# Sixteen batched matmuls: casting loads on GpSimd's queue, replaced by plain fp32 loads and stores on one hardware queue with casts on VectorE

## The chip, the cores and the metric

The kernel runs on one NeuronCore of a Trainium2 chip. The metric is the device time of one execution in microseconds. Three executions of the kernel before took 276.04, 276.12 and 276.22 us; their median is 276.12 us. The profiled execution has a span of 276.1 us from its first to its last instruction.

Engine names in the profile: PE is TensorE (PEld its weight loads), DVE is VectorE, ACT is ScalarE, POOL is GpSimd, SP is SyncE. A trailing "q" (SPq, POOLq) means the sequencer of an engine, which issues DMAs. L49 is line 49 of the kernel file.

## The reference

```python
def setup_inputs():
    batch, m, k, n = 16, 512, 768, 1024
    return {
        "x": np.random.randn(batch, k, m).astype(np.float32),
        "y": np.random.randn(batch, k, n).astype(np.float32),
    }

def reference(x, y):
    return np.einsum('bkm,bkn->bmn', x, y).astype(np.float32)
```

For each of 16 batches, x (768 x 512) is contracted with y (768 x 1024) over the first axis, and the result is 512 x 1024, all of it fp32 in HBM. Per batch 1.573 MB of x and 3.146 MB of y are read and 2.097 MB of the result are written: 6.816 MB, and 109.05 MB over the 16 batches. The sum over k may be taken in any order, so any assignment of the 768 rows to partitions is allowed as long as x and y have the same one.

## The kernel before

The matmuls run in bf16 with fp32 sums in PSUM. K = 768 is cut into KT = 6 slices of 128 rows, M = 512 into MT = 4 tiles of 128, N = 1024 into NT = 2 tiles of 512. One batch is 6 x 4 x 2 = 48 matmuls of 128x512, each with its own weight load of 128x128.

**Loads.** GpSimd issues four DMAs for each batch (L62 and L64, two halves of three K slices of x and of y). They read fp32 rows from HBM and cast to bf16 on the way into SBUF. Row ko*128 + p goes to partition p, so a contiguous run of x is one row of 512 elements (2 KB in HBM, 1 KB in SBUF), and one of y a row of 1024 elements (4 KB and 2 KB). x_sb and y_sb have four buffers each, so loads run up to four batches ahead.

**Matmuls.** With K_OUTER the loop over K slices is the outer one: all eight PSUM banks of a batch are open at the same time, and the 48 matmuls go through them six times (L49, called from L73). The first bank is complete only after most of the batch.

**Copies and stores.** When a batch's matmuls are done, its eight PSUM banks are copied to SBUF as fp32, alternately by VectorE and ScalarE (L78). After every second copy SyncE issues a store of one 128 x 1024 tile (512 KB, L79), in which a contiguous run is one output row of 4 KB. So there are four stores per batch, on SyncE's hardware queue, beside the loads on GpSimd's software queue. Both queues are served by the same 16 DMA engines.

The order is the scheduler's; on each engine the instructions stand in program order, and each DMA waits on its issuing queue for the semaphores it needs.

Of the kernel before, what the change touches and what calls it, by code (L numbers as in the profile page):

```python
# [1 line left out]

_os.environ.setdefault("NEURON_RT_ULTRASERVER_MODE", "4")

# [1 line left out]

# [4 lines left out]

LOAD_SPLIT = 2
K_OUTER = True


@with_exitstack
def kernel(
    ctx: ExitStack,
    tc: tile.TileContext,  # L20
    x: bass.AP,
    y: bass.AP,
    out: bass.AP,
):
    nc = tc.nc
    P = 128
    FP32 = mybir.dt.float32
    BF16 = mybir.dt.bfloat16

    B, K, M = x.shape  # L30
    _, _, N = y.shape

    KT = K // P
    MT = M // P
    NF = 512
    NT = N // NF
    KC = KT // LOAD_SPLIT

    x_v = x.rearrange("b (ko p) m -> b ko p m", p=P)
    y_v = y.rearrange("b (ko p) n -> b ko p n", p=P)  # L40
    o_v = out.rearrange("b (mo p) n -> b mo p n", p=P)

    x_pool = ctx.enter_context(tc.tile_pool(name="x_pool", bufs=4))
    y_pool = ctx.enter_context(tc.tile_pool(name="y_pool", bufs=4))
    o_pool = ctx.enter_context(tc.tile_pool(name="o_pool", bufs=12))
    psum = ctx.enter_context(tc.tile_pool(name="psum", bufs=8, space=bass.MemoryType.PSUM))

    def mm(ps, x_sb, y_sb, kt, mt, nt):
        nc.tensor.matmul(  # L49
            ps[:],  # L50
            x_sb[:, kt, mt * P:(mt + 1) * P],
            y_sb[:, kt, nt * NF:(nt + 1) * NF],
            start=(kt == 0),
            stop=(kt == KT - 1),
        )

    for b in range(B):
        x_sb = x_pool.tile([P, KT, M], BF16, name="x_sb")
        y_sb = y_pool.tile([P, KT, N], BF16, name="y_sb")
        for c in range(LOAD_SPLIT):  # L60
            ks = slice(c * KC, (c + 1) * KC)
            nc.gpsimd.dma_start(  # L62
                x_sb[:, ks], x_v[b, ks].rearrange("ko p m -> p ko m"))
            nc.gpsimd.dma_start(  # L64
                y_sb[:, ks], y_v[b, ks].rearrange("ko p n -> p ko n"))

        o_sb = [o_pool.tile([P, N], FP32, name="o_sb") for _ in range(MT)]
        ps = [psum.tile([P, NF], FP32, name="ps") for _ in range(MT * NT)]
        if K_OUTER:
            for kt in range(KT):  # L70
                for mt in range(MT):
                    for nt in range(NT):
                        mm(ps[mt * NT + nt], x_sb, y_sb, kt, mt, nt)  # L73
            for mt in range(MT):
                for nt in range(NT):
                    j = mt * NT + nt
                    eng = nc.vector.tensor_copy if j % 2 == 0 else nc.scalar.copy
                    eng(o_sb[mt][:, nt * NF:(nt + 1) * NF], ps[j][:])  # L78
                nc.sync.dma_start(o_v[b, mt], o_sb[mt][:])  # L79
        else:  # L80
            for mt in range(MT):
                for nt in range(NT):
                    j = mt * NT + nt
                    for kt in range(KT):
                        mm(ps[j], x_sb, y_sb, kt, mt, nt)
                    eng = nc.vector.tensor_copy if j % 2 == 0 else nc.scalar.copy
                    eng(o_sb[mt][:, nt * NF:(nt + 1) * NF], ps[j][:])
                nc.sync.dma_start(o_v[b, mt], o_sb[mt][:])


# [1 line left out]
_INS = ['x', 'y']  # L92
_OUTS = [((16, 512, 1024), 'float32')]


# [23 lines left out]
```

## Time and profile before

| | |
|---|---|
| median of three executions | 276.12 us |
| span of the profiled execution | 276.1 us |
| PE busy | 192.3 us (70%), 753 matmuls recorded of 768 |
| DVE / ACT busy | 39.7 us (14%) / 34.1 us (12%) |
| software queue q0 (casting loads) | 25600 packets, 37.75 MB written to SBUF, 75.7% of 16 engines' span |
| hardware queue q1 (stores) | 9216 packets, 33.56 MB, 32.2% |
| HBM read / written | 75.50 MB / 33.55 MB |
| mean granted TensorE clock | 0.895 |

The queue rows count bytes on the side that is written. A casting load reads twice what it writes, so the 37.75 MB of q0 are 75.50 MB read from HBM. To compare rates before and after, a GB/s number of a stretch with loads has to be brought back to HBM bytes: times 2 where only loads run, and times 109.05/71.31 = 1.529 in the steady mixture of loads and stores (71.31 MB is the sum of q0 and q1). Shares of a queue can add up to more than 100%, because the time of one packet overlaps that of the next one on the same engine.

### The profile page before, as it was taken

The page shows a single profiled execution, that of the slowest core. Times are in us where ns is not written, and L with a number is a line of the kernel's source. Part 1 is how long each engine was busy: PE and PEld are TensorE (multiplying, and loading weights), DVE is VectorE, ACT ScalarE, POOL GpSimd, SP SyncE. Part 2 cuts the span into 40 slices and gives each one's busy share as a digit, 9 for nine tenths or more (in the row PEclk, how much of TensorE's full clock was granted, in tenths as well). Part 3 has the DMA queues.
Part 4 walks back from the last instruction along what each step waited for, and adds up shares of the span by engine and source line. Part 5 has one row for each costly group of instructions (what it writes and reads, how often), then busy time and mean ns, then how long its engine had stood idle before and what let it go on. Part 6 is the DMA issues. An engine that isn't in the chain of part 4 may idle for free.

```text
span 276.1 us, 2127 instructions
## 1 busy us (share of the span) xinstructions
PE 192.3 (70%) x753; PEld 79.9 (29%) x768; DVE 39.7 (14%) x64; ACT 34.1 (12%) x65; POOL 49.8 (18%) x68
## 2 busy tenths in 40 slices
PE   0599727698278788495784993769919695849770
PEld 0144313243133333132331441324403332313330
DVE  0003110033003003030300303003030030302011
ACT  1002110022002002020200202002020020202011
POOL 8422121221212122121212311122112221000000
PEclk9999977799689979889978898689986998997997
DMA  5999999999999999999999999999999999999937
GB/s 92 202 208 237 317 279 284 208 243 315 296 268 210 284 279 245 315 210 297 260 294 267 211 302 286 319 216 209 320 291 302 209 252 309 223 315 233 283 156 304
DMA packets 34826, 71.44 MB, mean 259 GB/s; under 512 B 2048, under 2 KB 14336, under 8 KB 34816
## 3 DMA queue, kind: packets, MB, share of 16 engines
q0 software_dynamic: 25600, 37.75, 75.7%
q1 hardware_dynamic: 9216, 33.56, 32.2%
q8 instruction: 6, 0.10, 0.1%
q14 instruction: 4, 0.03, 0.0%
HBM read 75.50 MB, written 33.55 MB: 395 GB/s over the span
## 4 chain that ended last, share of the span: by engine, by line
DMA 90%; issue 3%; POOL 2%; PE 2%; DVE 0%; DVEq 0%; POOLq 0%
DMA x_sb<-in_x_dram 78%; DMA y_sb<-in_y_dram 12%; PE ps L49 2%; POOL x_sb L62 1%; POOL y_sb L64 1%; DVE o_sb L78 0%; DVEq L114 0%; DVEq L78 0%; POOLq L114 0%; POOLq L103 0%
## 5 line engine op out<-in xcount | busy, mean ns | idle before, releaser
L49 PE MATMUL ps<-y_sb,x_sb 128*128 128x512 bf16 x753 | 192.3, 416 | 77.0 <-DMA y_sb<-in_y_dram 72.3
L49 PEld LDWEIGHTS <-x_sb 128*128 128x128 bf16 x768 | 79.9, 105 | 188.8 <-issue 109.9
L78 DVE COPY o_sb<-ps 128x512 f32<-128x512 f32 x64 | 39.7, 683 | 230.6 <-issue 167.7
L78 ACT COPY o_sb<-ps 128x512 f32<-128x512 f32 x64 | 32.9, 600 | 235.2 <-issue 172.9
L64 POOL DMA_DIRECT2D y_sb<-in_y_dram x32 | 24.7, 773 | 105.2 <-DMA y_sb<-in_y_dram 105.2
L62 POOL DMA_DIRECT2D x_sb<-in_x_dram x32 | 24.8, 777 | 76.5 <-DMA x_sb<-in_x_dram 70.7
L78 ACT ACT_TABLE_LOAD x1 | 1.3, 1283 | 0.7 <-PEq L103 0.7
L103 POOL MEMSET const-float32-0.0<- 128x1 f32 x1 | 0.1, 93 | 0.2 <-issue 0.2
L103 POOL MEMSET const-bfloat16-1.0<- 128x1 bf16 x1 | 0.1, 95 | 0.0
L103 POOL MEMSET const-float32-1.0<- 128x1 f32 x1 | 0.1, 93 | 0.0
L103 POOL MEMSET const-uint8-127<- 128x1 uint8 x1 | 0.1, 93 | 0.0
## 6 DMA issues: line engine op xcount, KB each, us to landing
out_dram<-o_sb SPq DMA_DIRECT2D x64, 512.0 KB, 8.9
y_sb<-in_y_dram POOLq DMA_DIRECT2D x32, 768.0 KB, 32.9
x_sb<-in_x_dram POOLq DMA_DIRECT2D x32, 384.0 KB, 32.8
```

Source lines behind the costliest of these rows:

```text
L49: nc.tensor.matmul(ps[:], x_sb[:, kt, mt * P:(mt + 1) * P], y_sb[:, kt, nt * NF:(nt + 1) * NF], start=(kt == 0), stop=(kt == KT - 1),)
L62: nc.gpsimd.dma_start(x_sb[:, ks], x_v[b, ks].rearrange("ko p m -> p ko m"))
L64: nc.gpsimd.dma_start(y_sb[:, ks], y_v[b, ks].rearrange("ko p n -> p ko n"))
L78: eng(o_sb[mt][:, nt * NF:(nt + 1) * NF], ps[j][:])
L103: nc = _bacc.Bacc("TRN2", target_bir_lowering=False, num_devices=1)
```

## The change

The change rewrites how data gets in and out, and hands the cast to an engine.

- **Loads** are plain fp32 DMAs into staging tiles xs and ys (two buffers each), one DMA for x and one for y per batch, issued by SyncE (L56, L57). Row p*6 + ko goes to partition p, so each partition reads one contiguous run: 12 KB of x, 24 KB of y.
- **Casts** to bf16 are on VectorE: one for x (L62) and two halves for y (L65), each 128 x 3072 elements. x_sb and y_sb now have two buffers each.
- **Matmuls** (L74) have the K slices innermost, one PSUM bank at a time. Weights are taken at a step of four elements (x_w, L66), so that output row j*4 + mo lands on partition j, and a partition's four output rows are one contiguous run of 16 KB.
- **PSUM copies** are all on ScalarE (L76), into an o_sb tile of a whole batch, of which there are five.
- **Stores** are one DMA per batch (L50, 2 MB), on the same SyncE queue as the loads, and batch b-4 is stored right behind the loads of batch b. The last four batches are stored after the last loads.
- The order is fixed by hand (`tc.manual_schedule()`): every engine runs its instructions as written.

```diff
-    x_v = x.rearrange("b (ko p) m -> b ko p m", p=P)
-    y_v = y.rearrange("b (ko p) n -> b ko p n", p=P)
-    o_v = out.rearrange("b (mo p) n -> b mo p n", p=P)
-    x_pool = ctx.enter_context(tc.tile_pool(name="x_pool", bufs=4))
-    y_pool = ctx.enter_context(tc.tile_pool(name="y_pool", bufs=4))
-    o_pool = ctx.enter_context(tc.tile_pool(name="o_pool", bufs=12))
+    x_v = x.rearrange("b (p ko) m -> b p ko m", ko=KT)
+    y_v = y.rearrange("b (p ko) n -> b p ko n", ko=KT)
+    o_v = out.rearrange("b (p mo) n -> b p mo n", mo=MT)
+    xs_pool = ctx.enter_context(tc.tile_pool(name="xs_pool", bufs=2))
+    ys_pool = ctx.enter_context(tc.tile_pool(name="ys_pool", bufs=2))
+    x_pool = ctx.enter_context(tc.tile_pool(name="x_pool", bufs=2))
+    y_pool = ctx.enter_context(tc.tile_pool(name="y_pool", bufs=2))
+    o_pool = ctx.enter_context(tc.tile_pool(name="o_pool", bufs=5))
+    LAG = 4
...
+    def store(b):
+        nc.sync.dma_start(o_v[b], o_tiles.pop(b)[:])
+
+    with tc.manual_schedule():
+        for b in range(B):
+            xs = xs_pool.tile([P, KT, M], FP32, name="xs")
+            ys = ys_pool.tile([P, KT, N], FP32, name="ys")
+            nc.sync.dma_start(xs[:], x_v[b])
+            nc.sync.dma_start(ys[:], y_v[b])
+            if b >= LAG:
+                store(b - LAG)
+            x_sb = x_pool.tile([P, KT, M], BF16, name="x_sb")
+            y_sb = y_pool.tile([P, KT, N], BF16, name="y_sb")
+            nc.vector.tensor_copy(x_sb[:], xs[:])
+            for h in range(2):
+                ks = slice(h * KT // 2, (h + 1) * KT // 2)
+                nc.vector.tensor_copy(y_sb[:, ks], ys[:, ks])
+            x_w = x_sb[:].rearrange("p k (j mo) -> p k mo j", mo=MT)
+            o_sb = o_pool.tile([P, MT, N], FP32, name="o_sb")
+            o_tiles[b] = o_sb
+            for mo in range(MT):
+                for nt in range(NT):
+                    ns = slice(nt * NF, (nt + 1) * NF)
+                    ps = psum.tile([P, NF], FP32, name="ps")
+                    for kt in range(KT):
+                        nc.tensor.matmul(ps[:], x_w[:, kt, mo], y_sb[:, kt, ns],
+                                         start=(kt == 0), stop=(kt == KT - 1))
+                    nc.scalar.copy(o_sb[:, mo, ns], ps[:])
...
+        for b in sorted(o_tiles):
+            store(b)
```

How the order of the instructions changes is seen at three places. In the rows, DMAHW and DMASW are semaphores that a DMA raises when it has landed (eight of each kind, used in turn), and DVE, PE and Activation are those of the engines.

The first place is the middle of the program on the queues that issue DMAs. Before, GpSimd issues the loads of two batches like this, with none of the stores among them:

```order
L62 DMA x_sb_379<-in_x_dram 128x3x512 [waits DMASW0_49,PE_49]
L64 DMA y_sb_380<-in_y_dram 128x3x1024 [waits DMASW1_49]
L62 DMA x_sb_379<-in_x_dram 128x3x512 [waits DMASW2_49]
L64 DMA y_sb_380<-in_y_dram 128x3x1024 [waits DMASW3_49]
L62 DMA x_sb_457<-in_x_dram 128x3x512 [waits DMASW4_49,PE_49]
L64 DMA y_sb_458<-in_y_dram 128x3x1024 [waits DMASW5_49]
```

A load there waits for the one eight DMAs earlier, whose semaphore it reuses, and at the start of a batch for TensorE to be done with the buffer. With the change, SyncE's queue holds everything; here are the loads of batches 4 and 5 and the stores of batches 0 and 1:

```order
L56 DMA xs_371<-in_x_dram 128x3072 [waits DMAHW4_49,DVE_49]
L57 DMA ys_372<-in_y_dram 128x6144 [waits DMAHW5_49,DVE_49]
L50 DMA out_0_dram<-o_sb_84 128x4096 [waits Activation_49]
L56 DMA xs_446<-in_x_dram 128x3072 [waits DMAHW6_49,DVE_49]
L57 DMA ys_447<-in_y_dram 128x6144 [waits DMAHW7_49,DVE_49]
L50 DMA out_0_dram<-o_sb_158 128x4096 [waits Activation_49]
```

A load now waits for VectorE to have cast the batch two before out of the same staging buffer, and a store, which waits for ScalarE's copies of the batch four before, stands between the loads.

The second place is the end of SyncE's queue with the change: the last loads (batch 15) and the stores of batches 11 to 15.

```order
L56 DMA xs_1196<-in_x_dram 128x3072 [waits DMAHW3_49,DVE_49]
L57 DMA ys_1197<-in_y_dram 128x6144 [waits DMAHW4_49,DMAHW2_49,DVE_49]
L50 DMA out_0_dram<-o_sb_906 128x4096 [waits Activation_49]
L50 DMA out_0_dram<-o_sb_981 128x4096 [waits Activation_49]
L50 DMA out_0_dram<-o_sb_1056 128x4096 [waits DMAHW5_49,Activation_49]
L50 DMA out_0_dram<-o_sb_1131 128x4096 [waits DMAHW6_49,Activation_49]
L50 DMA out_0_dram<-o_sb_1206 128x4096 [waits DMAHW7_49,Activation_49]
```

Five whole batches' stores now stand behind the last load; before, it was the stores of the batch just computed.

The third place is the start of a batch's casts on VectorE with the change (batches 1 and 2), where before there were only copies out of PSUM:

```order
L62 CAST x_sb_153<-xs_149 128x3072 [waits DMAHW2_49]
L65 CAST y_sb_154<-ys_150 128x3072 [waits DMAHW3_49]
L65 CAST y_sb_154<-ys_150 128x3072
L62 CAST x_sb_227<-xs_223 128x3072 [waits DMAHW4_49,DVE_49,PE_49]
L65 CAST y_sb_228<-ys_224 128x3072 [waits DMAHW5_49,DVE_49]
```

A cast waits for its load to have landed, and from the third batch on for TensorE to be done with the bf16 buffer of the batch two before.

More of the change, by code (lines that the diff above doesn't have):

```diff
@@ L11 @@
 from concourse._compat import with_exitstack
-LOAD_SPLIT = 2
-K_OUTER = True
 @with_exitstack
@@ L36 @@
     NT = N // NF
-    KC = KT // LOAD_SPLIT
-    x_v = x.rearrange("b (ko p) m -> b ko p m", p=P)
-    y_v = y.rearrange("b (ko p) n -> b ko p n", p=P)
-    o_v = out.rearrange("b (mo p) n -> b mo p n", p=P)
-    x_pool = ctx.enter_context(tc.tile_pool(name="x_pool", bufs=4))
-    y_pool = ctx.enter_context(tc.tile_pool(name="y_pool", bufs=4))
-    o_pool = ctx.enter_context(tc.tile_pool(name="o_pool", bufs=12))
-    psum = ctx.enter_context(tc.tile_pool(name="psum", bufs=8, space=bass.MemoryType.PSUM))
@@ L48, in mm @@
[L48 to L74, printed above, removed]
-                for nt in range(NT):
[L76 to L83, printed above, removed]
-                    for kt in range(KT):
[L85 to L88, printed above, removed]
@@ new lines @@
+    psum = ctx.enter_context(tc.tile_pool(name="psum", bufs=8, space=bass.MemoryType.PSUM))
+    LAG = 4
+    o_tiles = {}
+    def store(b):
[18 more added lines that the diff above has]
+            for mo in range(MT):
+                for nt in range(NT):
+                    ns = slice(nt * NF, (nt + 1) * NF)
+                    ps = psum.tile([P, NF], FP32, name="ps")
+                    for kt in range(KT):
+                        nc.tensor.matmul(ps[:], x_w[:, kt, mo], y_sb[:, kt, ns],
+                                         start=(kt == 0), stop=(kt == KT - 1))
+                    nc.scalar.copy(o_sb[:, mo, ns], ps[:])
+            if False:
+                store(b)
+        for b in sorted(o_tiles):
+            store(b)
```

## The prediction

> **What bounds the kernel now.** I read the page first: busy shares, DMA rows, queues, and the shares of the chain of waits.
>
> ```profile
> span 276.1 us, 2127 instructions
> ...
> PE 192.3 (70%) x753; PEld 79.9 (29%) x768; DVE 39.7 (14%) x64; ACT 34.1 (12%) x65; POOL 49.8 (18%) x68
> ...
> DMA  5999999999999999999999999999999999999937
> ...
> DMA packets 34826, 71.44 MB, mean 259 GB/s; under 512 B 2048, under 2 KB 14336, under 8 KB 34816
> ...
> q0 software_dynamic: 25600, 37.75, 75.7%
> q1 hardware_dynamic: 9216, 33.56, 32.2%
> q8 instruction: 6, 0.10, 0.1%
> ...
> HBM read 75.50 MB, written 33.55 MB: 395 GB/s over the span
> ...
> DMA 90%; issue 3%; POOL 2%; PE 2%; DVE 0%; DVEq 0%; POOLq 0%
> ```
>
> The DMA engines are busy in every slice but the first and the last two, and 90% of the chain that ended last is DMA. TensorE is busy in 70% of the span. The kernel moves 109.05 MB of HBM data and is bound by moving it, so two things matter: the rate while the DMA engines work, and how long they stand still. The next view cuts the span into stretches (columns: length, busy time of PE, PEld, DVE, ACT and POOL, PE clock, DMA share, GB/s by written bytes).
>
> ```profile
> 12.00:20.00 8.00, 8.00 (x35) 3.50 (x34) 0.00 (x0) 0.00 (x0) 2.32 (x3) 1.00 1.14 208
> 40.00:238.00 198.00, 146.26 (x564) 60.17 (x573) 29.00 (x47) 24.08 (x48) 35.95 (x47) 0.88 1.12 267
> ...
> 270.00:274.00 4.00, 0.00 (x0) 0.00 (x0) 0.29 (x1) 0.07 (x1) 0.00 (x0) 0.87 1.02 406
> ```
>
> *Rate.* From 12 to 20 us only loads run: 208 GB/s written, 416 read. From 270 to 274 only stores: 406. In the steady middle 267 x 1.529 = 408 GB/s of HBM bytes. All three are within 3%, on one queue or on two.
>
> *Standing still.* The same view at the two ends of the program, and the rows of the timeline that belong to it:
>
> ```profile
> 3.00:4.00 1.00, 0.00 (x0) 0.00 (x0) 0.00 (x0) 0.00 (x0) 1.00 (x2) 1.00 0.26 40
> 4.00:5.00 1.00, 0.00 (x0) 0.00 (x0) 0.00 (x0) 0.00 (x0) 1.00 (x2) 1.00 1.20 199
> ```
> ```profile
> 264.00:266.00 2.00, 2.00 (x10) 0.87 (x9) 0.00 (x0) 0.00 (x0) 0.00 (x0) 1.00 0.46 188
> 266.00:268.00 2.00, 1.95 (x10) 0.89 (x10) 0.19 (x1) 0.00 (x0) 0.00 (x0) 1.00 0.00 0
> 268.00:269.00 1.00, 1.00 (x6) 0.38 (x4) 1.00 (x2) 0.98 (x3) 0.00 (x0) 1.00 0.00 0
> 269.00:270.00 1.00, 0.23 (x2) 0.00 (x0) 1.00 (x3) 1.00 (x3) 0.00 (x0) 1.00 0.57 229
> ...
> 274.00:275.00 1.00, 0.00 (x0) 0.00 (x0) 0.00 (x0) 0.00 (x0) 0.00 (x0) 0.50 0.64 246
> ```
> ```profile
> 0.73 1.28 ACT L78 ACT_TABLE_LOAD   x1 [0.73 <-PEq L103]
> 1.24 0.89 POOL L62 DMA_DIRECT2D x_sb<-in_x_dram  x1 [0.80 <-POOLq L103]
> ```
> ```profile
> 263.89 5.34 PE L49 MATMUL ps<-y_sb,x_sb 128*128 128x512 bf16 x23 [3.08 <-DMA y_sb<-in_y_dram]
> ```
> ```profile
> 268.63 2.88 SPq L79 DMA_DIRECT2D out_dram<-o_sb  x4
> ```
>
> Load data begins at about 3.75 us (share 0.26 in the fourth microsecond). The last load has landed at 263.9; stores of the batch before run on until 264.9 (0.46 of two us). Then nothing moves until 269.43 (share 0.57), because the last 23 matmuls and the copies come first. The last stores end at 274.64, the span at 276.1. Idle: 3.75 + 4.5 + 1.4 = 9.7 us, which leaves 266.4 us for 109.05 MB: 409 GB/s, the steady rate again. So **276.1 = 266.4 of transfer + 9.7 idle**, and this span is the median 276.12 within 0.02, so nothing has to be added.
>
> **The change part by part.**
>
> *Bytes.* None are removed: 75.50 MB in, 33.55 MB out. The casting DMA had to read fp32 too.
>
> *Idle ends.* Head: SyncE can issue from about 0.73, when the other engines have left the start-up barrier (the table load's row). Its last group of stores was issued at 268.63 and moved at 269.43, 0.8 us later; GpSimd's first load took 3.75 - 1.24 = 2.5. With SyncE's nearer to 0.8, and something for HBM reads, I take 1.3: data at 2.0 instead of 3.75. Tail: after the last load the queue holds stores 11 to 14, 8.39 MB, some 19.6 us of transfer at the rate found below. Meanwhile the last batch needs two y casts, 48 matmuls at 146.26/564 = 0.259 us (12.4), one copy, and 0.8 from issue to data. The prices of these:
>
> ```profile
> L49 PE MATMUL ps<-y_sb,x_sb 128*128 128x512 bf16 x753 | 192.3, 416 | 77.0 <-DMA y_sb<-in_y_dram 72.3
> L49 PEld LDWEIGHTS <-x_sb 128*128 128x128 bf16 x768 | 79.9, 105 | 188.8 <-issue 109.9
> L78 DVE COPY o_sb<-ps 128x512 f32<-128x512 f32 x64 | 39.7, 683 | 230.6 <-issue 167.7
> L78 ACT COPY o_sb<-ps 128x512 f32<-128x512 f32 x64 | 32.9, 600 | 235.2 <-issue 172.9
> ```
>
> A cast is 128x3072. No row shows one; six times the 683 ns of a 512-wide copy gives 4.1 us as its upper bound, and nothing is the lower one. Then the last store is ready 13.8 to 22.0 us after y lands, against 19.6 us of stores that cover it (up to 1.4 less, as landing is seen late): a gap of 0 to 3.8 us. I take 1.5. The Trainium skill, "VectorE: DVE Perf Modes", section on the perf-mode tier table, gives 1227 ns for an fp32 copy of 2048 elements within SBUF; an estimate of 1.8 us per cast from it would close the gap, and the forecast would be 257.4. No row before shows it.
>
> The 1.4 us after the last byte stay.
>
> *Other engines in the steady part.* VectorE: three casts, at most 12.3 us per batch. ScalarE: eight copies, 4.8. TensorE: 12.4. Each is under the 15.9 us that a batch's transfers will take, so they cost nothing while the queue stays filled. Does it? SyncE stops at the y load of batch b until batch b-2 is cast out of its buffer. When y of b-2 lands, its queue still holds a store, the loads of b-1, another store and the x load of b: 2.1 + 4.7 + 2.1 + 1.6 = 10.5 MB, some 24 us, against 8.2 us for two casts at most. The x loads wait for an x cast a whole batch old. A store four behind waits for copies that ended over two batches ago; so nothing is stuck behind it. GpSimd's 64 DMA issues leave no mark: it was mostly waiting for landings.
>
> *Rate.* The page has no data packet over 4 KB: 25600 and 9216 packets for rows of 1, 2 and 4 KB as written. With the change a run is 12, 24 or 16 KB. What a packet costs beside its bytes comes from two stretches at the start, the first with x packets alone (2 KB read), the second with y packets alone (4 KB read). First from 3.5 to 5.5 us:
>
> ```profile
> DMA packets 315, 0.32 MB, mean 161 GB/s; under 512 B 0, under 2 KB 315, under 8 KB 315
> ...
> q0 software_dynamic: 315, 0.32, 98.0%
> ```
> Then from 7 to 9 us:
> ```profile
> DMA packets 205, 0.42 MB, mean 210 GB/s; under 512 B 0, under 2 KB 0, under 8 KB 205
> ...
> q0 software_dynamic: 205, 0.42, 112.2%
> ```
>
> A packet took 0.980 x 2 us x 16 / 315 = 99.6 ns and 1.122 x 32 / 205 = 175.1 ns. 2048 more bytes cost 75.5 ns: 27.1 GB/s per engine, 434 for 16. In throughput a y packet took 4096 B x 16 / 420 GB/s (twice 210) = 156.1 ns, of which 151.0 are its bytes: 5 ns of its own. A store packet at 406 GB/s took 161.4: 10 ns. If a run stays whole, an engine with eight partitions needs per batch 8 x (453 + 5 + 906 + 5 + 604 + 10) ns = 15.87 us, and 16 batches 254 us (429 GB/s). If runs are cut at 4 KB, 9 pieces of 156.1 and 4 of 161.4 ns per partition give 262.5; at the unchanged steady rate it is 266.4. These are the bounds, 254 to 266. The q8 row has 0.10 MB in 6 packets, 16 KB each: longer packets do exist. I take the whole run.
>
> **Sum:** 254.0 transfer + 2.0 head + 1.4 end + 1.5 tail gap = **259 us**, of its own 256 to 264 (two short stretches fix the rate to about 2%).
>
> **The rivals.**
>
> *A: the runs don't help.* Runs are cut into short packets, or the 408 GB/s are a limit that no packet size moves. For it: loads, stores and mixture agree within 3%, though their packets differ. Against it: the price per packet above. Time: 262.5 to 266.4 plus 3.4 idle, 266 to 270. The Trainium skill ("DMA: Bandwidth & Descriptors", section "SWDGE vs HWDGE vs iDMA") wants packets of at most 4096 B and so stands on this side; the q8 row is against a hard limit. Chance 0.32.
>
> *B: TensorE becomes the bound (slower).* Weights are now read at a step of four elements. Place: LDWEIGHTS, 105 ns, today beside the matmuls. If it can no longer be hidden, a matmul takes 259 + 105 = 364 ns. TensorE starts when y of batch 0 is cast, about 18 us in (2.0 + 4.72 MB at 429 + 1.4 + casts), and 7.7 us follow it (copy, issue, 4.9 for a store, 1.4): 768 x 0.364 + 25.7 = 305 us. It decides from 327 ns per matmul. Against it: weight loads are busy for 29% only, so even a doubled one fits beside a matmul. Chance 0.06.
>
> *C: gaps between DMAs in a single queue (slower from a point on).* With one queue nothing fills a gap at the hand-over from one DMA to the next. If each of 48 costs the 0.8 us from issue to data, 257.4 + 38 = 296; slower than before from 0.39 us each. Against it: the 12 to 20 us and 270 to 274 us stretches run on one queue over several DMAs at 416 and 406. Chance 0.05.
>
> *D: a cap on HBM traffic (slower).* Reads and writes of the core are held below what the steady row shows: slower from 109.05 MB / 272.7 us = 400 GB/s down. The rows are against it, 395 over the whole span with 9.7 us idle. The Trainium skill ("HBM Reference", specifications) gives about 358 GB/s as effective per core; an estimate by that is 308 us, and the trace disagrees by its 395. Chance 0.02.
>
> *E: no change,* gains eaten by some of these. Chance 0.03.
>
> **How the numbers follow.** The forecast has the remaining 0.52. Within 0.2% (0.55 us) is what can't be told from no change. Faster: forecast and A, with a little of C, 0.86. Slower: B, D and most of C, 0.11. The range 256 to 271 joins the forecast's own with A's, and leaves out about 0.15.
>
> **What would show it.** Right: the queues row with 109 MB on the hardware queue, a packet count far below 34826, a steady rate over 420 GB/s, DMA as the chain, and SyncE's issue always ahead. A: packets all 4 KB or less and 408 to 415 GB/s. B: LDWEIGHTS well over 105 ns and matmuls waiting for nothing. C: holes in the DMA row at each hand-over. The tail step fails if the DMA share drops for more than 4 us before the last store. A cast above 4.1 us would break the cover of the steady part.

## The result, and the profile after

The changed kernel takes **261.98 us** (median of four executions, 261.81 to 262.44), against 276.17 us for the kernel before (276.04 to 276.52, four executions). The ratio is 0.9481, with a 95% interval of 0.9459 to 0.9503. Six later executions of the change gave a median of 261.98 us again. Two executions that were over 1.5% above the fastest of their kernel (278.49 us with short stores, 302.02 us with stores one batch behind) are left out of the medians below.

The profiled execution of the change took 261.84 us with a span of 260.1 us. Every execution whose span and time are both known, of every kernel here, lies about 1.7 to 2.0 us above its span; the kernel before had 275.89 us with 274.1, and 277.58 with 275.8. The spans are what the profiles below can explain. The profiled execution of the kernel before, with its span of 276.1 us, must by this have taken about 277.9 us, 1.7 more than the median of 276.17. In three later sets beside the experiments the kernel before ran between 275.89 and 279.47 us, with medians of 277.49 to 277.56.

The page of the changed kernel:

```profile
span 260.1 us, 1877 instructions
...
PE 192.3 (74%) x768; PEld 89.3 (34%) x768; DVE 83.0 (32%) x48; ACT 76.4 (29%) x129; POOL 0.2 (0%) x4
...
DMA  7999999999999999999999999999999999999995
...
DMA packets 6921, 109.18 MB, mean 420 GB/s; under 512 B 768, under 2 KB 768, under 8 KB 768
...
q1 hardware_dynamic: 6912, 109.05, 98.5%
...
HBM read 75.50 MB, written 33.55 MB: 419 GB/s over the span
...
DMA 80%; DVE 10%; PE 5%; DVEq 1%; SPq 0%; issue 0%; ACT 0%
...
L74 PEld LDWEIGHTS <-x_sb 128*128 128x128 bf16 x768 | 89.3, 118 | 160.9 <-issue 47.5
L76 ACT COPY o_sb<-ps 128x512 f32<-128x512 f32 x128 | 75.2, 587 | 174.1 <-PE ps L74 174.1
L65 DVE CAST y_sb<-ys 128x3072 bf16<-128x3072 f32 x32 | 54.9, 1757 | 89.4 <-DMA ys<-in_y_dram 89.4
```

The bytes are the same, but 34826 packets have become 6921. Of the 6912 on the hardware queue 768 are completion marks of 4 bytes, 16 for each of the 48 DMAs; the other 6144 are 128 partitions x 3 DMAs x 16 batches, so every run of 12, 16 or 24 KB went as one packet. DMA is still the bound; only the last slice is half empty.

The chain of waits (start, length, what; in us) shows how regular the steady part is:

```profile
112.04 28.08 DMA ys<-in_y_dram
...
143.68 28.08 DMA ys<-in_y_dram
...
206.94 28.08 DMA ys<-in_y_dram
```

The chain comes back to the same place every 31.64 us, which is two batches: 15.82 us per batch. VectorE has 10% of the chain, as a y load is issued when a cast frees its buffer; this costs nothing: taken packet by packet, at least 16 packets are in work, as many as there are DMA engines, in over 99% of the time from 60 to 220 us. Stretches of the span, with the same columns as before:

```profile
0.00:2.00 2.00, 0.00 (x0) 0.00 (x0) 0.00 (x0) 1.28 (x1) 0.20 (x4) 1.00 0.26 49
2.00:4.00 2.00, 0.00 (x0) 0.00 (x0) 0.00 (x0) 0.01 (x1) 0.00 (x0) 1.00 0.76 295
...
60.00:220.00 160.00, 123.77 (x489) 56.57 (x487) 52.60 (x31) 48.13 (x82) 0.00 (x0) 0.89 1.01 430
```
```profile
251.00:252.00 1.00, 0.00 (x0) 0.00 (x0) 0.00 (x0) 0.29 (x1) 0.00 (x0) 1.00 0.66 279
252.00:253.00 1.00, 0.00 (x0) 0.00 (x0) 0.00 (x0) 0.00 (x0) 0.00 (x0) 1.00 1.19 508
...
256.00:257.00 1.00, 0.00 (x0) 0.00 (x0) 0.00 (x0) 0.00 (x0) 0.00 (x0) 0.50 0.77 328
257.00:258.00 1.00, 0.00 (x0) 0.00 (x0) 0.00 (x0) 0.00 (x0) 0.00 (x0) 0.50 0.43 180
258.00:259.00 1.00, 0.00 (x0) 0.00 (x0) 0.00 (x0) 0.00 (x0) 0.00 (x0) 0.50 0.04 16
```

A packet counts in the window in which it starts, so with packets of 0.46 to 0.91 us the shares of windows of one microsecond swing about 1.

The steady rate is 430 GB/s, now without any factor, since nothing is cast on the way. In the first 4 us the DMA engines lose 4 - 2 x (0.26 + 0.76) = 1.96 us. From 256 us to the end they lose 4.1 - (0.77 + 0.43 + 0.04) = 2.9 us. That leaves 260.1 - 4.8 = 255.3 us of transfer, against 266.4 before. So of the 16.0 us by which the span shrank, **11.1 are rate and 4.9 are time in which the DMA engines stood still at the two ends**. This holds for the two profiled executions; the medians are only 14.2 us apart, and as no quicker execution of the kernel before has a profile, it is open which of the two parts is smaller there.

### The profile page after: what moved, and what is told of

It reads as the page before. It is cut to its first block, busy times and chain, and to the rows that moved or that the text cites. A ratio compares the mean times of both kernels' runs of the same rounds, so it can differ in the third digit from the quotient of the medians.

```text
span 260.1 us, 1877 instructions
## 1 busy us (share of the span) xinstructions
PE 192.3 (74%) x768; PEld 89.3 (34%) x768; DVE 83.0 (32%) x48; ACT 76.4 (29%) x129; POOL 0.2 (0%) x4
## 3 DMA queue, kind: packets, MB, share of 16 engines
q1 hardware_dynamic: 6912, 109.05, 98.5%
## 4 chain that ended last, share of the span: by engine, by line
DMA 80%; DVE 10%; PE 5%; DVEq 1%; SPq 0%; issue 0%; ACT 0%
DMA ys<-in_y_dram 80%; DVE y_sb L65 10%; PE ps L74 5%; DVEq L106 1%; SPq L56 0%; ACT o_sb L76 0%; SPq L57 0%; DVEq L65 0%
## 5 line engine op out<-in xcount | busy, mean ns | idle before, releaser
L74 PE MATMUL ps<-y_sb,x_sb 128*128 128x512 bf16 x768 | 192.3, 413 | 58.4 <-DVE y_sb L65 58.4
L74 PEld LDWEIGHTS <-x_sb 128*128 128x128 bf16 x768 | 89.3, 118 | 160.9 <-issue 47.5
L76 ACT COPY o_sb<-ps 128x512 f32<-128x512 f32 x128 | 75.2, 587 | 174.1 <-PE ps L74 174.1
L65 DVE CAST y_sb<-ys 128x3072 bf16<-128x3072 f32 x32 | 54.9, 1757 | 89.4 <-DMA ys<-in_y_dram 89.4
L62 DVE CAST x_sb<-xs 128x3072 bf16<-128x3072 f32 x16 | 28.2, 1760 | 66.2 <-DMA xs<-in_x_dram 55.2
```

The source lines that it names most:

```text
L62: nc.vector.tensor_copy(x_sb[:], xs[:])
L65: nc.vector.tensor_copy(y_sb[:, ks], ys[:, ks])
L74: nc.tensor.matmul(ps[:], x_w[:, kt, mo], y_sb[:, kt, ns], start=(kt == 0), stop=(kt == KT - 1))
L76: nc.scalar.copy(o_sb[:, mo, ns], ps[:])
```

## The experiments

The theory was: whole runs make packets cheaper (the rate), the early start and the stores kept back for the end take away idle time (the ends), and nothing else matters. The rivals were that the rate came from dropping the cast or the software queue, and that the order or the single queue played another part.

### Run lengths put back in the changed kernel

```diff
-    x_v = x.rearrange("b (p ko) m -> b p ko m", ko=KT)
-    y_v = y.rearrange("b (p ko) n -> b p ko n", ko=KT)
-    o_v = out.rearrange("b (p mo) n -> b p mo n", mo=MT)
+    x_v = x.rearrange("b (ko p) m -> b p ko m", p=P)
+    y_v = y.rearrange("b (ko p) n -> b p ko n", p=P)
+    o_v = out.rearrange("b (mo p) n -> b p mo n", p=P)
...
-            x_w = x_sb[:].rearrange("p k (j mo) -> p k mo j", mo=MT)
+            x_w = x_sb[:].rearrange("p k (mo j) -> p k mo j", mo=MT)
```

> The change with only the run lengths put back: rows of x (2 KB), y (4 KB) and the result (4 KB) are dealt to the partitions as before, weights are contiguous again; queue, order, casts and copies stay as changed. Theory (a packet costs 5 to 10 ns beside its bytes, so whole runs carry the gain in rate): per batch an engine needs 8 x (6 x 80.5 + 6 x 156.1 + 4 x 161.4) ns = 16.5 us, 264 us in all or 412 GB/s, 10 us more than the change: 272 us. Rival (the gain in rate comes from the plain hardware-queue DMA without a cast, whatever the runs): steady rate stays near 428 GB/s and the time near 262 us.

Measured: 273.25 us (273.20 to 273.63). The page's packet row and the window from 40 to 220 us:

```profile
DMA packets 33545, 109.18 MB, mean 402 GB/s; under 512 B 768, under 2 KB 768, under 8 KB 33536
```
```profile
40.00:220.00 180.00, 136.46 (x543) 55.53 (x541) 60.51 (x35) 52.70 (x90) 0.00 (x0) 0.89 1.03 411
```

The expected rate was 412 GB/s and the measured one is 411; the time is 11.3 us above the change. The rival falls: a plain DMA without a cast on the hardware queue is no faster in itself. Of the 14.2 us between the medians before and after, the run lengths account for 11.3; all else in the change together is worth the other 2.9.

Another reading would be that SyncE can't issue short runs fast enough. It does need longer for them, where 0.33 us was enough in the change (start, length, what):

```profile
105.25 7.43 SPq L57 DMA_DIRECT2D ys<-in_y_dram  x1
112.73 5.22 SPq L50 DMA_DIRECT2D out_dram<-o_sb  x1
```

But the DMA engines don't wait for it: their share is 1.03 in the window above, and at least 16 packets are in work in over 99% of the time from 60 to 220 us.

### Longer runs alone in the kernel before

```diff
-    x_v = x.rearrange("b (ko p) m -> b ko p m", p=P)
-    y_v = y.rearrange("b (ko p) n -> b ko p n", p=P)
+    x_v = x.rearrange("b (p ko) m -> b p ko m", ko=KT)
+    y_v = y.rearrange("b (p ko) n -> b p ko n", ko=KT)
...
-                x_sb[:, ks], x_v[b, ks].rearrange("ko p m -> p ko m"))
+                x_sb[:, ks], x_v[b, :, ks])
...
-                y_sb[:, ks], y_v[b, ks].rearrange("ko p n -> p ko n"))
+                y_sb[:, ks], y_v[b, :, ks])
```

> The kernel before with only the loads' rows dealt so that a partition's three rows of a half are contiguous (6 KB of x, 12 KB of y in HBM); casting DMAs on GpSimd's queue, stores of 4 KB rows and the scheduler's order stay. Theory (run length): 8 x (2 x 231.6 + 2 x 458 + 4 x 161.4) ns = 16.2 us per batch, 259 us, plus the 9.7 us idle of the kernel before: 269 us, a half of the change's gain. Rival (the cast or the software queue holds the rate down): 276 us, no change.

Measured: 271.97 us (271.90 to 272.00), span 270.2; the kernel before beside it had 275.89 to 279.30 us. The rival's 276 us is out. Its windows, steady part and end:

```profile
40.00:220.00 180.00, 133.11 (x532) 54.74 (x530) 27.33 (x44) 22.59 (x44) 23.28 (x45) 0.91 1.05 274
...
260.00:262.00 2.00, 2.00 (x11) 0.94 (x10) 0.02 (x1) 0.00 (x0) 0.00 (x0) 1.00 0.08 31
262.00:264.00 2.00, 1.40 (x7) 0.43 (x5) 2.00 (x4) 1.82 (x4) 0.00 (x0) 1.00 0.20 80
```

In HBM bytes the steady rate is 274 x 1.529 = 419 GB/s (the sum said 421), up from 408, on the software queue and with the cast. The span is 1.3 us over the 268.9 of the sum, as much as those 2 GB/s make. The hole at the end, which this kernel keeps, costs 3.4 us in the last two rows. The rate stays under the 427 GB/s that plain whole-run loads reach beside the same stores (below); whether the shorter runs of 6 and 12 KB, the cast or the software queue hold it back there, no run separates.

### Which of the runs carry the price

Only the stores' runs put back (o_v and x_w of the first diff), and only the loads' (x_v and y_v); the change itself ran beside them on the same chip.

> The change itself once more, so that the next three stand beside it on the same chip. Every theory: 262 us, as measured before.

> The change with only the stores' runs put back to output rows of 4 KB (weights contiguous again), loads in whole runs. Theory (5 ns for each load packet, 10 ns for each store packet): 4 x 161.4 instead of 614 ns per partition and batch, 31.6 ns x 128 = 4.0 us more than the change: 266 us. Rival (the price of short runs is on the HBM reads alone): 262 us.

> The change with only the loads' runs put back to rows of 2 KB and 4 KB, stores in whole runs. Theory: 6 x (80.5 + 156.1) instead of 458 + 911 ns per partition and batch, 50.6 ns x 128 = 6.5 us more than the change: 268.5 us, and with the stores' 4.0 this adds up to the 11 us of both together. Rival (price on the stores alone): 262 us.

Measured: the change 261.98 us (261.73 to 262.39), short stores 263.5 (263.23 to 263.65), short loads 272.33 (271.92 to 272.75). The sum of the two is right, 1.5 + 10.4 = 11.9 against 11.3 for both, but the share of each is not: 4.0 and 6.5 were expected. A short store costs 1.5 us / (8 partitions x 3 more packets x 16 batches = 384) = 4 ns more, a short load 10.4 us / (8 x 10 x 16 = 1280) = 8 ns. The steady part with short stores:

```profile
60.00:220.00 160.00, 125.94 (x478) 50.81 (x485) 51.89 (x31) 48.08 (x82) 0.00 (x0) 0.86 1.01 427
```

The windows of the kernel with short loads, the first with loads alone:

```profile
12.00:20.00 8.00, 2.52 (x6) 0.81 (x6) 3.93 (x3) 0.00 (x0) 0.00 (x0) 1.00 1.04 397
...
60.00:220.00 160.00, 120.44 (x464) 54.80 (x472) 50.13 (x29) 46.07 (x79) 0.00 (x0) 0.87 1.03 413
```

The rows of x and y that the casting DMA read at 416 GB/s from 12 to 20 us go at 397 as plain fp32. The mix differs (768 packets of x and 392 of y here, 384 and 619 there), but by the prices of the prediction that is only 3 of the 19 GB/s. So the price measured on casting loads was too low for plain ones; the queue differs as well as the cast, and no run tells which of them matters.

### Stores two, three and one batch behind

```diff
-    LAG = 4
+    LAG = 2
```

> The change with stores two batches behind instead of four. Theory (stores left over at the end cover the last batch's casts, matmuls and copies, nothing else depends on the lag): two stores less of cover, 2 x 4.9 us, so the DMA engines stand still some 10 us before the last store and the time is 272 us; the steady rate stays at 428 GB/s. Rival (the lag does not matter at the end, for the last store is ready in time anyway): 262 us. A second rival (a lag of two already blocks the loads behind a waiting store in the steady part): above 275 us, with holes in every batch.

> The change with stores three batches behind. Theory (what is left in the queue behind the last load must cover the 16.3 us from its landing to the issue of the last store; with four behind the slowest DMA engine never runs dry, with two behind the loss was 9 us): one store less of cover than the change, 4.9 us, less what was to spare: 265 to 267 us. Rival (two behind lost its 9 us in the steady part, not at the end): 262 us.

> The change with stores one batch behind. Theory: a store now waits on SyncE's queue for a batch whose y has just landed, and the next loads wait behind it, so two batches take at least 17 us from landing to the store's data plus 15.9 us of transfer, 16.5 us per batch or more instead of 15.8; with another store's 4.9 us missing at the end the time is 285 us or more, above the kernel before, and the DMA row has a hole in every batch. Rival (loads run far enough ahead that only the end counts): 276 us.

Measured: 271.01 us (270.25 to 271.80) for two, 265.55 (263.99 to 266.34) for three, 299.78 (297.38 to 301.47) for one. The windows of the kernel with two:

```profile
40.00:220.00 180.00, 133.57 (x540) 62.14 (x539) 58.10 (x34) 52.78 (x90) 0.00 (x0) 0.91 1.01 430
...
250.00:255.00 5.00, 5.00 (x15) 1.75 (x14) 0.00 (x0) 1.24 (x3) 0.00 (x0) 0.55 0.47 200
255.00:260.00 5.00, 5.00 (x25) 2.64 (x24) 0.00 (x0) 2.27 (x4) 0.00 (x0) 1.00 0.00 0
260.00:265.00 5.00, 1.37 (x7) 0.48 (x5) 0.00 (x0) 1.17 (x2) 0.00 (x0) 0.97 0.50 210
```

The steady rate is unchanged; on the mean of the 16, the DMA engines stand still from about 252.4 to 262.5 us, waiting for the last batch. From four to two the time rises by 9.0 us, from four to three by 3.6, both as expected. With one batch behind the steady part breaks as well. SyncE's queue there (start, length, what), and the steady window:

```profile
100.96 0.34 SPq L50 DMA_DIRECT2D out_dram<-o_sb  x1
101.40 0.38 SPq L56 DMA_DIRECT2D xs<-in_x_dram  x1
101.89 0.85 SPq L57 DMA_DIRECT2D ys<-in_y_dram  x1
118.16 0.34 SPq L50 DMA_DIRECT2D out_dram<-o_sb  x1
118.59 0.38 SPq L56 DMA_DIRECT2D xs<-in_x_dram  x1
```
```profile
40.00:220.00 180.00, 124.16 (x463) 55.88 (x474) 53.66 (x31) 45.73 (x78) 0.00 (x0) 0.83 0.95 387
```

The loads stand behind the waiting store and are issued right after it, 17.2 us apart in these rows (17.4 on the mean from 101 to 258 us) instead of 15.8, so the rate drops to 387 GB/s. The direction and the place were as expected; the loss is larger than the least that was given (285 us).

### Stores on ScalarE's queue, at once

```diff
-            if b >= LAG:
-                store(b - LAG)
...
-        nc.sync.dma_start(o_v[b], o_tiles.pop(b)[:])
+        nc.scalar.dma_start(o_v[b], o_tiles.pop(b)[:])
...
-            if False:
-                store(b)
+            store(b)
```

> The change with the stores on ScalarE's hardware queue, each issued as soon as its batch is copied, and only loads on SyncE's queue. Theory (the DMA engines give the same rate to one queue or two; what the fixed order buys is the cover at the end): steady rate 428 GB/s, but behind the last load only what is left of one store, so 10 to 14 us stand still at the end: 272 to 276 us. Rival (a single queue loses time at each hand-over, about 1 us was seen lost at the first store): the steady rate rises above 432 GB/s and a part of the loss at the end comes back, 268 us or less.

Measured: 273.55 us (273.15 to 273.71).

```profile
40.00:220.00 180.00, 136.63 (x531) 62.06 (x532) 59.83 (x35) 51.61 (x88) 0.00 (x0) 0.88 1.01 431
...
255.00:260.00 5.00, 5.00 (x23) 2.41 (x21) 0.00 (x0) 1.76 (x4) 0.00 (x0) 0.93 0.00 0
260.00:265.00 5.00, 3.85 (x18) 1.81 (x16) 0.00 (x0) 2.34 (x4) 0.00 (x0) 1.00 0.00 0
```

The rate is 431 GB/s with two queues and 430 with one, so a single queue loses nothing that can be told at its hand-overs. What issuing the stores at once on a second queue changes is the end: no store is left to cover the last batch, and over 10 us stand empty.

### The last store in two halves

```diff
         for b in sorted(o_tiles):
-            store(b)
+            if b == B - 1:
+                o_sb = o_tiles.pop(b)
+                for h in range(2):
+                    ms = slice(h * MT // 2, (h + 1) * MT // 2)
+                    nc.sync.dma_start(o_v[b, :, ms], o_sb[:, ms])
+            else:
+                store(b)
```

> The change with the very last store cut in two halves of 8 KB runs, so that the first half can go when four of eight copies are done. Theory (about 0.5 us of standing still before the last store, and nothing else wrong at the end): 261.5 us. Rival (the end is set by engines that finish at different times, and the hole before the last store is a part of that): 262 us, no difference that can be told.

Measured: 262.05 us (261.70 to 262.21), beside 261.98 for the change: no difference that can be told. Its windows at the end:

```profile
251.00:252.00 1.00, 0.00 (x0) 0.00 (x0) 0.00 (x0) 0.00 (x0) 0.00 (x0) 1.00 0.91 385
...
256.00:257.00 1.00, 0.00 (x0) 0.00 (x0) 0.00 (x0) 0.00 (x0) 0.00 (x0) 0.50 0.66 279
257.00:258.00 1.00, 0.00 (x0) 0.00 (x0) 0.00 (x0) 0.00 (x0) 0.00 (x0) 0.50 0.29 123
258.00:259.00 1.00, 0.00 (x0) 0.00 (x0) 0.00 (x0) 0.00 (x0) 0.00 (x0) 0.50 0.08 33
```

The hole before the last store is gone (0.91 instead of 0.66 in that microsecond), but the last data come no sooner. The 16 completion marks of the last store show why. In the change they arrive from 257.43 to 259.24 us, here from 256.12 to 259.47: the engines that had run dry were ahead and now finish earlier, and the last ones had never been held up. The rival holds. No version that was run beats the change by anything that can be told.

## Why the prediction was right, step by step

**The forecast's mechanism held**: 259 us were predicted, 261.98 measured, with the range 256 to 271. What rival A rests on, packets cut to 4 KB or a limit of 408 GB/s, did not happen.

**Rate (254.0 us predicted).** In the steady part 15.82 us per batch against 15.87, 430 GB/s against 429. Over the whole run the transfer took 255.3. That the sum over loads and stores came out this well is partly luck: the experiments with one kind of run each show that the load price (5 ns) was too low and the store price (10 ns) too high. The 5 ns came from casting loads; plain loads pay about 8 ns for each extra packet. The 10 ns came from four small stores at the end of the kernel before, and in the steady mixture it was 4. Whole runs make both small, so the forecast did not hang on them; the prices for kernels in between did.

The Trainium skill ("DMA: Bandwidth & Descriptors", section "SWDGE vs HWDGE vs iDMA") prefers packets of at most 4096 B where it describes the software queue. The prediction counted this for rival A; on the hardware queue of this case longer packets pay: with packets of 12 to 24 KB the kernel is 11.3 us faster than with 2 to 4 KB.

**Head (2.0 us predicted).** 1.96 us lost in the first four; SyncE issues at 0.73 us, as predicted.

**End (1.4 + 1.5 us predicted).** The sum, 2.9, came out as measured, but by luck: the gap of 1.5 us was of another kind and size. The rows that speak for it, from the timeline of the change:

```profile
235.12 3.43 DVE L65 CAST y_sb<-ys 128x3072 bf16<-128x3072 f32 x2 [5.50 <-DMA ys<-in_y_dram]
```
```profile
251.32 0.33 SPq L50 DMA_DIRECT2D out_dram<-o_sb  x1
```

A cast took 1757 ns, well within the bounds of 0 and 4.1 us. The estimate of 1.8 us that the prediction worked out from the Trainium skill ("VectorE: DVE Perf Modes", the perf-mode tier table) agrees.

The last store was issued 16.2 us after the last load was seen landed, where the sum with this cast gives 17.3 less 0.8 for the data to move. By the sum that leaves no gap, and yet the share fell to 0.66 at 251 us. The completion marks of the last y load come in from 231.95 to 235.03 us: the engine that was ahead had turned to the stores 3.1 us before the landing was seen, not 1.4. Packet by packet the engines lose 0.35 us there on the mean, and the split store showed that this costs nothing. What takes the place of the gap is a term that the prediction put at nothing, the uneven finish: 1.2 us on the mean of the engines from 256 us to the last data at 258.85. From there to the end of the span it is 1.2 us more, near the 1.4 predicted.

**Outside the span (nothing predicted).** This is the step that failed: the prediction took the profiled span of 276.1 us for a time that agrees with the median of 276.12 and added nothing. All executions lie 1.7 to 2.0 us above their spans. On that ground the forecast should have read 259 + 1.75 = 260.8. The remaining 1.2 us are 255.3 instead of 254.0 us of transfer.

**Rivals.** *TensorE:* reading the weights at a step of four made LDWEIGHTS 118 ns instead of 105 (104 with contiguous weights in the run with short runs), and it stays beside the matmuls. *Gaps in a single queue:* refuted by 430 GB/s on one queue and 431 on two. *A cap on HBM traffic:* refuted by 419 GB/s over the span. The Trainium skill ("HBM Reference", specifications), which the prediction cited for about 358 GB/s per core, also says there that a core streaming alone measures well above this share, and the trace agrees with it. *The x and y casts, ScalarE's copies:* 83.0 and 76.4 us busy in a span of 260, hidden.

**What SyncE's order is worth.** The prediction's argument on the waits held at a lag of four, and the runs show where it ends: with a lag of one the loads do queue up behind a waiting store, and the kernel is slower than before the change.

## What to carry to other kernels

When DMA engines are busy all the time, split the time into transfer and standstill, and get the price of a packet from two stretches with packets of different length; that told in advance what longer contiguous runs would bring. In a queue with a fixed order, keep back enough stores to cover the last batch's computation, but put none in front of loads unless its data is long ready. Compare a span with the time of the same execution before using it as that time.

## What the runs showed of the hardware that was not expected

A plain fp32 load in rows of 2 and 4 KB ran at 397 GB/s, while the casting load of the same rows ran at 416 read; 3 of the 19 GB/s are the mix of rows.

The DMA engines drift apart within one queue: the 16 completion marks of one DMA spread over 3.0 us in the median of the change. Long packets are not the reason, for with all runs short the median spread is 2.9 us.

Around the first store of the change, whose first packet starts at 57.7 us, the rate falls for a few microseconds:

```profile
56.00:57.00 1.00, 1.00 (x6) 0.56 (x5) 0.00 (x0) 0.34 (x1) 0.00 (x0) 1.00 0.79 221
57.00:58.00 1.00, 1.00 (x7) 0.49 (x6) 0.00 (x0) 0.29 (x2) 0.00 (x0) 1.00 1.03 311
58.00:59.00 1.00, 1.00 (x6) 0.54 (x5) 0.00 (x0) 0.54 (x1) 0.00 (x0) 1.00 0.73 311
```

By its bytes this is about 1 us. The engines are not idle; the packets that start from 56 to 57.5 us, all of them 24 KB of the y load ahead of that store, are slow:

```profile
q1 hardware_dynamic: 16, 0.39, 95.0%
```

That is 0.950 x 1.5 us = 1.43 us for a packet, where the mean from 60 to 220 us is 0.91. With two batches behind the fall came at 34 to 37 us, where that kernel's first store begins (36.0 us); with short loads none was seen. Its cause is open, and so is whether it costs anything at the end.
